# Moving the combination of two attention maps to GpSimd, and delaying the last two gate sigmoids

## The chip, the cores and the metric

The kernel runs on one core of one Trainium2 chip. The metric is the device time of one launch in microseconds (us). Three runs of the kernel before took 1290.82, 1292.57 and 1293.42 us; the median, 1292.57 us, is what the changed kernel is set against.

Five engines matter. PE (TensorE) multiplies matrices into PSUM, with its weight loads shown as PEld. DVE (VectorE), ACT (ScalarE) and POOL (GpSimd) do the elementwise work. SP (SyncE) issues most of the DMAs. Each engine works through its own queue in order, and waits on semaphores that other engines or DMAs raise.

## The reference

One decoder block on x of 1024 tokens by 1024 channels, in float32. The part that the change touches:

```
z = rms_norm(x) @ w_in            -> p, q, k, v, gate_a, gate_b
for each of 4 heads, each block of 128 queries:
    s1 = q1 k1^T * scale + bias ; s2 = q2 k2^T * scale + bias   (causal)
    a  = softmax(s1) - lam * softmax(s2)
    o  = a @ v                                   (v: 128 columns)
    o  = o * rsqrt(mean(o^2) + eps) * subln_g * (1 - lambda_init)
ya = pool_mixer(p) @ w_branch_a ; yb = o_all_heads @ w_branch_b
m  = sigmoid(gate_a) * ya + sigmoid(gate_b) * yb
h  = x + rms_norm(m @ w_out)      then a SwiGLU feed-forward layer
```

## The kernel before, in words

Each float32 matrix product is made of three products of rounded halves (high by high, high by low, low by high); `triple` (lines 230 to 234) issues the three. The high half is an ACT cast, the low half a DVE or POOL subtraction (`sub`, line 87; `load_w`, line 97, uses POOL for the weights of the first branch).

The input projection comes first. It leaves q, k, v, the pooled activations and the gates in DRAM. The gates of channels 128d to 128d+127 are finished by `gate_done` (lines 511 to 519): a sigmoid on ACT for each half of the tokens, then a store from ACT's queue to `sgd[0][d]` (gate_a) or `sgd[1][d]` (gate_b). The last of the eight gate units, d = 7 (`KD - 1`), is not run at once. It becomes the first part of a *filler*: a generator whose steps are three matmuls each, and which goes on with the first branch (`branch(0, ...)`, pooled values by `w_branch_a`).

Attention runs over 32 entries, a head and a block of queries each, in the order of `seq` (line 712). The first three heads alternate long and short blocks (7, 0, 6, 1, 5, 2, 4, 3), the last goes down from 7 to 0. An entry of block qb has maps of 128 x L, L = 128 (qb + 1). It has three parts:

- `scores` (lines 599 to 633). For each of the two maps: matmuls into a PSUM pair; a DVE instruction (line 622) that adds the bias, writes the map `E` to SBUF and gives its row maximum; an exponential on ACT in place (line 625), whose accumulator gives the row sums. Then three DVE instructions (lines 629 to 631) take the reciprocals of the two sums, a factor cf from them, and `E[0] += cf * E[1]`.
- `transposes` (lines 638 to 652). PE transposes the 128 x 128 blocks of E[0] into PSUM (line 646); ACT and DVE make the two halves `AT` (lines 648 and 649).
- `values` (lines 654 to 669). PE multiplies by V (line 660); ACT and DVE scale the two column halves by the reciprocal of the first sum and add them (lines 665 to 667); ACT takes the sum of squares.

`head_norm` (lines 673 to 684) makes the head's norm factor on DVE and POOL (`rstd_of`, lines 121 to 126, a power of -0.5 on POOL) and multiplies on DVE (line 679). `turn_head` (lines 686 to 695) transposes the result for the second branch.

The loop at line 731 issues scores four entries ahead of the values, and transposes one ahead. After each step, `step` (lines 720 to 729) adds a pace to `owed` and issues that many filler steps. Outside the blocks marked `manual_schedule` the framework's scheduler then orders each engine's instructions from this order and from modelled durations; the result is fixed in each engine's queue.

`branch` (lines 576 to 592) takes 128 output channels (d) and 512 tokens (t) at a time: a gate load on SP into a temporary (line 587; two rotating buffers for each of the tags `ft` and `sg`), twelve matmuls into one of two PSUM banks (`fil`), then `take`. `take_a` multiplies by the gate into `ma`; `take_b` (lines 761 to 764) multiplies by the gate and adds `ma`. After the second branch the eight loads of `w_out` (line 776) are on SP too, with casts on ACT (line 777) and subtractions on DVE; they share two `wraw` buffers with the branch weights.

The long-lived tiles come from two pools: `a8` with 16 slots, and `b4` with 14 slots, which holds among others the maps E, the tiles AT and the four O.

Of the kernel before, what the change touches and what calls it, by code (L numbers as in the profile page):

```python
# [10 lines left out]
F32 = mybir.dt.float32  # L11
F32R = mybir.dt.float32r
AF = mybir.ActivationFunctionType
ALU = mybir.AluOpType

P = 128
S = 1024
D = 1024
NB = S // P
KD = D // P  # L20
HALF = 512
NH = 4
# [5 lines left out]
EPS = 1e-6  # L28
# [11 lines left out]
def block_kernel(ctx, tc, x, w_in, pool_mix, pool_scale, w_branch_a, lam_q1, lam_k1, lam_q2,  # L40
                 lam_k2, subln_g, w_branch_b, w_out, mix_pre_g, mix_post_g, ffn_pre_g, ffn_post_g,
                 w_ffn_gate, w_ffn_up, w_ffn_down, out):
    nc = tc.nc
    x, out = x[0], out[0]
# [7 lines left out]
    cp = ctx.enter_context(tc.tile_pool(name="cp", bufs=1))  # L52
# [8 lines left out]
    def name(s):  # L61
        uid[0] += 1
        return f"{s}_{uid[0]}"
# [4 lines left out]
    def b4(shape, dt, s):  # L68
        return sb.tile(shape, dt, tag="b4", bufs=B4, name=name(s))
# [4 lines left out]
    def fil(s):  # L74
        return ps.tile([P, HALF], F32, tag="fil", bufs=2, name=name(s))
# [4 lines left out]
    def small(n, s):  # L80
        return sm.tile([P, n], F32, tag="small", bufs=20, name=name(s))
# [31 lines left out]
    make_identity(nc, ident)  # L113
    mhalf = cp.tile([P, 8], F32, name="mhalf")
    nc.vector.memset(mhalf, -0.5)
    junk = cp.tile([P, D], mybir.dt.bfloat16, name="junk")
    psc = cp.tile([P, 4], F32, name="psc")
    sgc = cp.tile([P, 1], F32, name="sgc")
# [2 lines left out]
    def rstd_of(ss, n, width):  # L121

        t, r = small(n, "ms"), small(n, "rstd")
        nc.vector.tensor_scalar(t, ss, 1.0 / width, EPS, op0=ALU.mult, op1=ALU.add)
        nc.gpsimd.tensor_tensor(out=r, in0=t, in1=mhalf[:, :n], op=ALU.pow)
        return r
# [33 lines left out]
    def tt(o, a, b, op):  # L160
        nc.vector.tensor_tensor(out=o, in0=a, in1=b, op=op)  # L161
# [85 lines left out]
    def temp(s):  # L247
        if s in ("p1", "p5", "c11"):
            return sm.tile([P, HALF], F32, tag="ft", bufs=2, name=name(s))
        return sm.tile([P, HALF], F32, tag="sg", bufs=2, name=name(s))  # L250
# [43 lines left out]
    sgd = [[dr.tile([P, S], F32, name=name("sgd")) for _ in range(KD)] for _ in range(2)]  # L294

    def half(t):
        return slice(t * HALF, (t + 1) * HALF)
# [62 lines left out]
    with tc.manual_schedule(engines={nc.scalar.engine, nc.vector.engine, nc.gpsimd.engine}):  # L360
# [10 lines left out]
        o = [(fil("q"), fil("k")), (mm("q"), mm("k"))]  # L371
# [5 lines left out]
        for tb in range(NB):  # L377
            t, cols = tb // 4, slice(tb % 4 * P, (tb % 4 + 1) * P)
# [43 lines left out]
    for t in range(2):  # L422
        o = (fil("q"), fil("k")) if t == 0 else (mm("q"), mm("k"))
# [13 lines left out]
    lsum, lexp, nlam = small(2, "lsum"), small(2, "lexp"), cp.tile([P, 1], F32, name="nlam")  # L437
# [73 lines left out]
    def gate_done(d):  # L511
        st, seen = [b4([P, S], F32, "g_st") for _ in range(2)], [0, 0]

        def done(e, t, src):
            nc.scalar.activation(st[e][:, half(t)], src, AF.Sigmoid)
            seen[e] += 1
            if seen[e] == 2:
                nc.scalar.dma_start(sgd[e][d], st[e])
        return done
# [13 lines left out]
    heads, attends = {}, {}  # L533
# [42 lines left out]
    def branch(e, w, mov, take):  # L576

        order = [(d, t) for d in range(KD) for t in range(2)]
        if e == 1:
            order[:4] = [(0, 1), (1, 1), (0, 0), (1, 0)]  # L580
        ws = {}
        for d, t in order:
            if d not in ws:
                ws[d] = load_w(w[:, d * P:(d + 1) * P], 4, P, "wb", e == 0)
            bh, bl = ws[d]
            sg = temp(("p1", "sg")[t])
            nc.sync.dma_start(sg, sgd[e][d][:, half(t)])
            o = fil("branch")
            for k in range(4):
                triple(o, bh[:, k, :], bl[:, k, :], *mov(t, k), k == 0, k == 3, False)  # L590
                yield
            take(d, t, o, sg)

    ma = []

    def take_a(d, t, o, sg):
        tt(ma[t][d // 4][:, d % 4, :], o, sg, ALU.mult)

    def scores(h, qb):

        QA, QB, K, V = heads[h]
        slope = 0.25 ** (h + 1)
        L = P * (qb + 1)
        nj = 1 if L <= HALF else 2
        w = L // nj
        q = slice(qb * P, (qb + 1) * P)
        if nj == 1:
            E = b4([P, 2, HALF], F32, "E")
            E = [E[:, 0, :L], E[:, 1, :L]]
        else:  # L610
            E = [b4([P, S], F32, "E")[:, :L] for _ in range(2)]
        nm, sums = small(2, "nm"), small(2, "sums")
        dv = negd[:, S - L:S].rearrange("p (j w) -> p j w", j=nj)
        for m in range(2):
            sc = pair("s")
            for j in range(nj):
                c = slice(j * w, (j + 1) * w)
                nc.tensor.matmul(sc[:, j, :w], QA[:, m, q], K[:, m, c], start=True, stop=False)
                nc.tensor.matmul(sc[:, j, :w], QB[:, m, q], K[:, m, c], start=False, stop=True)
            e = E[m].rearrange("p (j w) -> p j w", j=nj)  # L620

            nc.vector.tensor_tensor_reduce(out=e, in0=sc[:, :nj, :w], in1=dv, scale=-slope,
                                           scalar=3.0e38, op0=ALU.add, op1=ALU.min,
                                           accum_out=nm[:, m:m + 1])
            nc.scalar.activation(E[m], E[m], AF.Exp, bias=nm[:, m:m + 1], scale=-1.0,
                                 accum_out=sums[:, m:m + 1])
            yield
        rec, cf = small(2, "rec"), small(1, "cf")
        nc.vector.reciprocal(rec, sums)
        nc.vector.tensor_scalar(cf, sums[:, 0:1], rec[:, 1:2], nlam, op0=ALU.mult, op1=ALU.mult)  # L630
        nc.vector.scalar_tensor_tensor(out=E[0], in0=E[1], scalar=cf, in1=E[0], op0=ALU.mult, op1=ALU.add)
        attends[h, qb] = E[0], rec
        yield

    O = [b4([P, NB, P], F32, "O") for _ in range(NH)]
    oss = [cp.tile([P, NB], F32, name=name("oss")) for _ in range(NH)]

    def transposes(h, qb):
        E, rec = attends[h, qb]
        ats = []  # L640
        for b0 in range(0, qb + 1, 4):
            n = min(4, qb + 1 - b0)
            pt = mm("aT")
            for i in range(n):
                b = b0 + i
                nc.tensor.transpose(pt[:, i * P:(i + 1) * P], E[:, b * P:(b + 1) * P], ident)
            AT = b4([P, 2, HALF], F32R, "AT")
            nc.scalar.copy(AT[:, 0, :n * P], pt[:, :n * P])
            sub(AT[:, 1, :n * P], pt[:, :n * P], AT[:, 0, :n * P])
            ats.append(AT)  # L650
            yield
        attends[h, qb] = ats, rec

    def values(h, qb):
        V = heads[h][3]
        ats, rec = attends[h, qb]
        o = mm("o")[:, :2 * P]
        for b in range(qb + 1):
            for j in range(2):
                nc.tensor.matmul(o, ats[b // 4][:, j, b % 4 * P:(b % 4 + 1) * P], V[:, b, :, :],  # L660
                                 start=b == 0 and j == 0, stop=b == qb and j == 1)
            if b == 3:
                yield
        ov = O[h][:, qb, :]
        nc.scalar.mul(ov, o[:, P:], rec[:, 0:1])
        nc.vector.scalar_tensor_tensor(out=ov, in0=o[:, :P], scalar=rec[:, 0:1], in1=ov,
                                       op0=ALU.mult, op1=ALU.add)
        sumsq(ov, oss[h][:, qb:qb + 1])
        yield

# [1 line left out]

    def head_norm(h, b=slice(0, NB)):
        n = b.stop - b.start
        r = rstd_of(oss[h][:, b], n, P)

        def scale():
            o = O[h][:, b, :]
            nc.vector.tensor_tensor(out=o, in0=o, in1=r.unsqueeze(2).to_broadcast([P, n, P]), op=ALU.mult)

        if h < NH - 1:
            defer(LAG, scale)
        else:
            scale()
# [46 lines left out]
    for i in range(-AHEAD, len(seq)):  # L731
        j = i + AHEAD
        if j < len(seq):
            h, pos = divmod(j, len(QORDER))
# [7 lines left out]
        if i >= 0:  # L742
            step(values(*seq[i]))
            h, pos = divmod(i, len(QORDER))
# [5 lines left out]
            elif h == NH - 1 and pos % 4 == 3:  # L750
                b = slice(4, 8) if pos == 3 else slice(0, 4)
# [6 lines left out]


    m = [[b4([P, 2, HALF], F32, "m") for _ in range(KD // 2)] for _ in range(2)]  # L760
    def take_b(d, t, o, sg):
        md = m[t][d // 2][:, d % 2, :]
        tt(md, o, sg, ALU.mult)
        tt(md, md, ma[t][d // 4][:, d % 4, :], ALU.add)

    for _ in branch(1, w_branch_b, quad_mov(OT), take_b):
        pass
# [130 lines left out]
    with tc.manual_schedule(engines={nc.tensor.engine, nc.scalar.engine, nc.vector.engine, nc.gpsimd.engine}):  # L898
        o = [fil("wo") for _ in range(2)]
# [9 lines left out]
        og, ss, ms, r = b4([P, D], F32, "og"), small(4, "hss"), small(4, "ms"), small(2, "rstd")  # L909
# [32 lines left out]
        for c in (c0, c1):  # L942
            nc.vector.scalar_tensor_tensor(out=xr[:, c], in0=og[:, c], scalar=r[:, 0:1], in1=xr[:, c],
                                           op0=ALU.mult, op1=ALU.add)
# [8 lines left out]
        for c in (c0, c1):  # L953
            nc.vector.scalar_tensor_tensor(out=og[:, c], in0=xr[:, c], scalar=r[:, 1:2], in1=gpre[:, c],
                                           op0=ALU.mult, op1=ALU.mult)
        sg = temp("sg")
# [22 lines left out]
    sg = temp("sg")  # L979
# [135 lines left out]
    for n, (i, kb) in enumerate(stream):  # L1115
# [8 lines left out]
        o = (Y, X, Y, X, Y, Z, Y)[i]  # L1124
# [40 lines left out]
```

## Time and profile before

| | us |
|---|---|
| median of three runs | 1292.57 |
| the profiled execution, its own time | 1293.83 |
| the span of its trace, first to last instruction | 1292.0 |
| PE busy, of the span | 1248.5 (97%) |
| DVE busy | 836.6 (65%) |
| ACT busy | 581.8 (45%) |
| POOL busy | 139.0 (11%) |

The attention stage, with the filler in it, lies at about 339 to 515 us of the span; the second branch follows until about 554 us, then the output projection and the feed-forward layer. Matmuls are pipelined and their ends are modelled, so PE counts as busy for some time after it could have taken the next matmul. A row of a busy view names line, engine, operation, output and inputs, shape and count, then busy time and the mean of one in ns, then the idle time of the engine just before and what ended it. A row of waits gives the total in us, how many, and the longest. A row of the timeline gives start, duration, engine, line, and in brackets how long the engine had been idle before and what ended that.

### The profile page before, as it was taken

The page shows a single profiled execution, that of the slowest core. Times are in us where ns is not written, and L with a number is a line of the kernel's source. Part 1 is how long each engine was busy: PE and PEld are TensorE (multiplying, and loading weights), DVE is VectorE, ACT ScalarE, POOL GpSimd, SP SyncE. Part 2 cuts the span into 40 slices and gives each one's busy share as a digit, 9 for nine tenths or more (in the row PEclk, how much of TensorE's full clock was granted, in tenths as well). Part 3 has the DMA queues.
Part 4 walks back from the last instruction along what each step waited for, and adds up shares of the span by engine and source line. Part 5 has one row for each costly group of instructions (what it writes and reads, how often), then busy time and mean ns, then how long its engine had stood idle before and what let it go on. Part 6 is the DMA issues. An engine that isn't in the chain of part 4 may idle for free.

```text
span 1292.0 us, 15663 instructions
## 1 busy us (share of the span) xinstructions
PE 1248.5 (97%) x5856; PEld 1038.3 (80%) x5856; DVE 836.6 (65%) x1303; ACT 581.8 (45%) x1033; POOL 139.0 (11%) x129
## 2 busy tenths in 40 slices
PE   4899999999989999999999999999999999999997
PEld 4788778888778887878878888888888888888886
DVE  4866685454369988655599565565566538865666
ACT  6444335344486666244564333333333334444542
POOL 3100000000101001001102111111110111000221
PEclk9899999999999999999999999999999999999999
DMA  7245246432598421543333323233223258733235
GB/s 248 66 159 183 100 152 197 131 118 86 173 307 221 139 73 43 168 160 131 112 106 114 105 91 101 96 122 123 86 86 114 98 197 307 242 101 91 89 107 203
DMA packets 139788, 179.16 MB, mean 139 GB/s; under 512 B 8000, under 2 KB 94528, under 8 KB 137280
## 3 DMA queue, kind: packets, MB, share of 16 engines
q1 hardware_dynamic: 127776, 146.56, 36.0%
q10 hardware_dynamic: 11936, 31.60, 6.3%
q8 instruction: 46, 0.75, 0.2%
q14 instruction: 30, 0.25, 0.1%
HBM read 124.39 MB, written 53.74 MB: 138 GB/s over the span
## 4 chain that ended last, share of the span: by engine, by line
PE 82%; DVE 7%; ACT 4%; DMA 3%; issue 2%; POOL 1%; ACTq 0%; SPq 0%; DVEq 0%; POOLq 0%
PE Y L232 9%; PE Y L233 9%; PE Y L234 9%; PE X L232 5%; PE X L233 5%; PE X L234 5%; PE Yd L233 3%; PE Yd L234 3%; PE Yd L232 3%; PE Z L233 2%; PE Z L234 2%; PE Z L232 2%; PE wo L818 2%; PE wo L819 2%; PE wo L817 2%
## 5 line engine op out<-in xcount | busy, mean ns | idle before, releaser
L161 DVE TENSOR_TENSOR p<-Z,p 128x512 f32<-128x512 f32 x35 | 24.2, 691 | 158.4 <-PE Z L234 158.4
L233 PE MATMUL Y<-A_lo,Wh 128*128 128x512 f32 x296 | 115.7, 391 | 0.3 <-DVE A_lo L87 0.3
L232 PE MATMUL Y<-A_hi,Wh 128*128 128x512 f32 x296 | 115.3, 390 | 0.0
L234 PE MATMUL Y<-A_hi,Wl 128*128 128x512 f32 x296 | 115.1, 389 | 0.0
L232 PE MATMUL Y<-S_hi,Wh 128*128 128x512 f32 x280 | 109.2, 390 | 0.0
L232 PE MATMUL X<-S_hi,Wh 128*128 128x512 f32 x280 | 109.1, 389 | 0.1
L233 PE MATMUL Y<-S_lo,Wh 128*128 128x512 f32 x280 | 109.1, 390 | 0.0
L234 PE MATMUL Y<-S_hi,Wl 128*128 128x512 f32 x280 | 109.1, 390 | 0.0
L234 PE MATMUL X<-S_hi,Wl 128*128 128x512 f32 x280 | 109.0, 389 | 0.0
L233 PE MATMUL X<-S_lo,Wh 128*128 128x512 f32 x280 | 109.0, 389 | 0.0
L201 ACT CAST Wh<-wf_t 128x1024 fp32r<-128x1024 f32 x70 | 72.8, 1053 | 69.2 <-PE X L233 30.7
L87 DVE TENSOR_TENSOR w_op<-wd,w_op 128x512 fp32r<-128x512 f32 x77 | 56.4, 732 | 55.2 <-ACT w_op L165 55.2
L87 DVE TENSOR_TENSOR Wl<-wf_t,Wh 128x1024 fp32r<-128x1024 f32 x70 | 86.6, 1244 | 4.6 <-ACT Wh L201 4.6
L201 ACT CAST Wh<-w_raw 128x1024 fp32r<-128x1024 f32 x72 | 60.6, 843 | 63.1 <-PE Z L233 41.9
L165 ACT CAST w_op<-wd 128x512 fp32r<-128x512 f32 x77 | 47.9, 622 | 89.1 <-PE Yd L234 34.4
L87 DVE TENSOR_TENSOR Wl<-w_raw,Wh 128x1024 fp32r<-128x1024 f32 x72 | 69.6, 966 | 14.5 <-ACT Wh L201 14.5
L233 PE MATMUL Yd<-w_op,s_op 128*128 128x512 f32 x176 | 68.7, 390 | 0.2 <-DVE w_op L87 0.2
L232 PE MATMUL Yd<-w_op,s_op 128*128 128x512 f32 x176 | 68.6, 390 | 0.0
L234 PE MATMUL Yd<-w_op,s_op 128*128 128x512 f32 x176 | 68.3, 389 | 0.0
L161 DVE TENSOR_TENSOR wf_t<-w_raw,wf_t 128x512 f32<-128x512 f32 x70 | 65.7, 938 | 1.0
L233 PEld LDWEIGHTS Y<-A_lo,Wh 128*128 128x128 f32 x296 | 55.6, 188 | 11.9 <-DVE A_lo L87 0.7
L232 PEld LDWEIGHTS Y<-A_hi,Wh 128*128 128x128 f32 x296 | 55.6, 188 | 11.6
(259 smaller groups left out, 3050.5 us busy)
## 6 DMA issues: line engine op xcount, KB each, us to landing
s_raw<-fsd SPq DMA_DIRECT2D x35, 512.0 KB, 3.7
w_raw<-in_w_in_dram SPq DMA_DIRECT2D x32, 512.0 KB, 4.0
w_raw<-in_w_ffn_gate_dram SPq DMA_DIRECT2D x22, 512.0 KB, 3.6
w_raw<-in_w_ffn_up_dram SPq DMA_DIRECT2D x22, 512.0 KB, 3.7
fsd<-fss SPq DMA_DIRECT2D x11, 1024.0 KB, 3.8
wd<-in_w_ffn_down_dram SPq DMA_DIRECT2D x44, 256.0 KB, 5.1
fsd<-F SPq DMA_DIRECT2D x33, 256.0 KB, 2.2
qkd<-qk_st ACTq DMA_DIRECT2D x16, 512.0 KB, 3.5
```

What stands on the lines that cost most here:

```text
L87: nc.vector.tensor_tensor(out=o, in0=a, in1=f32(hi), op=ALU.subtract)
L161: nc.vector.tensor_tensor(out=o, in0=a, in1=b, op=op)
L165: nc.scalar.copy(hi, a)
L201: nc.scalar.copy(hi, a)
L232: nc.tensor.matmul(o, ah, bh, start=start, stop=False, skip_group_check=goes_on)
L233: nc.tensor.matmul(o, ah, bl, start=False, stop=False, skip_group_check=goes_on)
L234: nc.tensor.matmul(o, al, bh, start=False, stop=stop, skip_group_check=goes_on)
L817: nc.tensor.matmul(o[e], mh[:, k, :], wh, start=k == 0, stop=False)
L818: nc.tensor.matmul(o[e], mh[:, k, :], wl, start=False, stop=False)
L819: nc.tensor.matmul(o[e], ml[:, k, :], wh, start=False, stop=k == KD - 1)
```

## The change

Combining the maps goes from DVE to POOL, in four instructions: a product for cf, a power of -1 for the reciprocal of the second sum, a multiplication of E[1] by both, an addition to E[0]. The values are no longer divided by the first sum; the sums are kept for each head (`esum`), and the norm takes eps times the squared first sum instead of eps, which gives the same normed result.

The last gates (d = 7) are stored as they are, by an ACT copy. The first branch does not load its gate for d = 7 and copies its product to `ma` on ACT. The second branch loads both gates for d = 7, takes both sigmoids on ACT in the temporaries, and multiplies `ma` by the first gate on DVE before the addition.

```diff
+    mone = cp.tile([P, 1], F32, name="mone")
+    nc.vector.memset(mone, -1.0)
...
         def done(e, t, src):
-            nc.scalar.activation(st[e][:, half(t)], src, AF.Sigmoid)
+            if d < KD - 1:
+                nc.scalar.activation(st[e][:, half(t)], src, AF.Sigmoid)
+            else:
+                nc.scalar.copy(st[e][:, half(t)], src)
...
-            sg = temp(("p1", "sg")[t])
-            nc.sync.dma_start(sg, sgd[e][d][:, half(t)])
+            gates = []
+            for i in ((0, 1) if d == KD - 1 else (e,)):
+                if d == KD - 1 and e == 0:
+                    continue
+                sg = temp(("p1", "sg")[t ^ (i != e)])
+                nc.sync.dma_start(sg, sgd[i][d][:, half(t)])
+                if d == KD - 1:
+                    nc.scalar.activation(sg, sg, AF.Sigmoid)
+                gates.append(sg)
...
-            take(d, t, o, sg)
+            take(d, t, o, gates)
...
-    def take_a(d, t, o, sg):
-        tt(ma[t][d // 4][:, d % 4, :], o, sg, ALU.mult)
+    def take_a(d, t, o, gates):
+        mad = ma[t][d // 4][:, d % 4, :]
+        if gates:
+            tt(mad, o, gates[0], ALU.mult)
+        else:
+            nc.scalar.copy(mad, o)
...
-        nm, sums = small(2, "nm"), small(2, "sums")
+        nm, sums = small(2, "nm"), esum[h][:, qb, :]
...
-        rec, cf = small(2, "rec"), small(1, "cf")
-        nc.vector.reciprocal(rec, sums)
-        nc.vector.tensor_scalar(cf, sums[:, 0:1], rec[:, 1:2], nlam, op0=ALU.mult, op1=ALU.mult)
-        nc.vector.scalar_tensor_tensor(out=E[0], in0=E[1], scalar=cf, in1=E[0], op0=ALU.mult, op1=ALU.add)
-        attends[h, qb] = E[0], rec
+        cf, rec = small(1, "cf"), small(1, "rec")
+        nc.gpsimd.tensor_tensor(out=cf, in0=sums[:, 0:1], in1=nlam, op=ALU.mult)
+        nc.gpsimd.tensor_tensor(out=rec, in0=sums[:, 1:2], in1=mone, op=ALU.pow)
+        nc.gpsimd.tensor_scalar(E[1], E[1], rec, cf, op0=ALU.mult, op1=ALU.mult)
+        nc.gpsimd.tensor_tensor(out=E[0], in0=E[0], in1=E[1], op=ALU.add)
+        attends[h, qb] = E[0]
...
-        nc.scalar.mul(ov, o[:, P:], rec[:, 0:1])
-        nc.vector.scalar_tensor_tensor(out=ov, in0=o[:, :P], scalar=rec[:, 0:1], in1=ov,
-                                       op0=ALU.mult, op1=ALU.add)
+        nc.scalar.copy(ov, o[:, P:])
+        tt(ov, o[:, :P], ov, ALU.add)
...
-        r = rstd_of(oss[h][:, b], n, P)
+        s0, t, r = esum[h][:, b, 0], small(n, "ms"), small(n, "rstd")
+        nc.vector.scalar_tensor_tensor(out=t, in0=s0, scalar=EPS, in1=s0, op0=ALU.mult, op1=ALU.mult)
+        nc.vector.scalar_tensor_tensor(out=t, in0=oss[h][:, b], scalar=1.0 / P, in1=t, op0=ALU.mult, op1=ALU.add)
+        nc.gpsimd.tensor_tensor(out=r, in0=t, in1=mhalf[:, :n], op=ALU.pow)
...
-    def take_b(d, t, o, sg):
-        md = m[t][d // 2][:, d % 2, :]
-        tt(md, o, sg, ALU.mult)
-        tt(md, md, ma[t][d // 4][:, d % 4, :], ALU.add)
+    def take_b(d, t, o, gates):
+        md, mad = m[t][d // 2][:, d % 2, :], ma[t][d // 4][:, d % 4, :]
+        tt(md, o, gates[-1], ALU.mult)
+        if len(gates) > 1:
+            tt(mad, mad, gates[0], ALU.mult)
+        tt(md, md, mad, ALU.add)
```

More of the change, by code (lines that the diff above doesn't have):

```diff
@@ L627, in scores @@
             yield
-        rec, cf = small(2, "rec"), small(1, "cf")
-        nc.vector.reciprocal(rec, sums)
-        nc.vector.tensor_scalar(cf, sums[:, 0:1], rec[:, 1:2], nlam, op0=ALU.mult, op1=ALU.mult)
-        nc.vector.scalar_tensor_tensor(out=E[0], in0=E[1], scalar=cf, in1=E[0], op0=ALU.mult, op1=ALU.add)
-        attends[h, qb] = E[0], rec
+        cf, rec = small(1, "cf"), small(1, "rec")
[4 more added lines that the diff above has]
+        attends[h, qb] = E[0]
         yield
+    esum = [cp.tile([P, NB, 2], F32, name=name("esum")) for _ in range(NH)]
     O = [b4([P, NB, P], F32, "O") for _ in range(NH)]
@@ L638, in transposes @@
     def transposes(h, qb):
-        E, rec = attends[h, qb]
+        E = attends[h, qb]
         ats = []
@@ L651, in transposes @@
             yield
-        attends[h, qb] = ats, rec
+        attends[h, qb] = ats
     def values(h, qb):
         V = heads[h][3]
-        ats, rec = attends[h, qb]
+        ats = attends[h, qb]
         o = mm("o")[:, :2 * P]
```

## The prediction

> **What bounds the kernel now.** I read the page first. It says that PE is the bound over the whole kernel, so an edit that takes work off DVE or ACT can only pay where PE waits for them.
>
> ```profile
> PE 1248.5 (97%) x5856; PEld 1038.3 (80%) x5856; DVE 836.6 (65%) x1303; ACT 581.8 (45%) x1033; POOL 139.0 (11%) x129
> ```
>
> The windows view then cuts out the attention stage and some stretches of it (columns: stretch, length, busy time of PE, PEld, DVE, ACT, POOL with counts, PE clock, DMA share, GB/s).
>
> ```profile
> 339.00:515.00 176.00, 167.13 (x974) 142.15 (x973) 142.21 (x351) 120.59 (x310) 21.00 (x15) 1.00 0.56 169
> ```
>
> ```profile
> 370.00:380.00 10.00, 8.45 (x49) 6.46 (x47) 5.86 (x15) 9.91 (x21) 0.93 (x1) 1.00 0.83 252
> 380.00:390.00 10.00, 7.57 (x44) 6.26 (x45) 8.97 (x27) 7.27 (x22) 1.04 (x1) 1.00 0.66 237
> 430.00:440.00 10.00, 8.17 (x52) 6.61 (x49) 9.01 (x26) 7.17 (x23) 0.00 (x0) 1.00 0.36 128
> 450.00:460.00 10.00, 10.00 (x59) 8.63 (x58) 9.56 (x27) 7.22 (x22) 1.31 (x1) 1.00 0.25 81
> ```
>
> PE idles 176.00 - 167.13 = 8.87 us in this stage, and 1.55 + 2.43 + 1.83 = 5.81 of it in three of these stretches: the first has ACT full, the others DVE near full. At 450 to 460, DVE is just as busy and PE loses nothing. So the prize is not DVE's share but these idle times, which PE's waits name:
>
> ```profile
> PE s L618 <- DVE nm L622: 3.0, 5, 1.0
> PE oT L692 <- DVE O L679: 1.3, 2, 0.9
> PE aT L646 <- DVE AT L87: 0.9, 2, 0.5
> PE aT L646 <- DVE O L666: 0.9, 2, 0.5
> ...
> PE o L660 <- DVE AT L87: 0.6, 1, 0.6
> PE o L660 <- DVE O L666: 0.5, 1, 0.5
> ```
>
> Those on steps that a freer DVE or ACT brings forward (L622, AT, L666) are 3.0 + 0.9 + 0.9 + 0.6 + 0.5 = 5.9 us in 11 waits. A wait costs a little more than it shows:
>
> ```profile
> 366.70 0.39 PE L233 MATMUL branch<-y2l,wb_hi 128*128 128x512 f32 x1
> 366.93 0.39 PE L234 MATMUL branch<-y2h,wb_lo 128*128 128x512 f32 x1
> ```
>
> Starts are 0.23 us apart while each matmul counts 0.39 as busy, so each wait hides 0.16 us more: 11 x 0.16 = 1.8. The most that the attention part can give is 7.7 us.
>
> **DVE loses the combination.** In the stage (group rows; last figures are busy us and mean ns):
>
> ```profile
> L631 DVE SCALAR_TENSOR_TENSOR E<-E,cf,E 128x1024 f32<-128x1024 f32 (+3 forms) x16 | 17.8, 1114 | 0.0
> L631 DVE SCALAR_TENSOR_TENSOR E<-E,cf 128x128 f32<-128x128 f32 (+3 forms) x16 | 8.7, 545 | 0.1
> L630 DVE TENSOR_SCALAR cf<-sums,rec,nlam 128x1 f32<-128x1 f32 x32 | 8.6, 269 | 0.7
> L629 DVE RECIPROCAL rec<-sums 128x2 f32<-128x2 f32 x32 | 5.2, 162 | 14.7 <-ACT E L625 14.1
> ```
>
> That is 40.3 us off 142.21, leaving about 102 in 176. The additions in `values` keep shape and place and are costed at nothing, as is the early memset, which lies beside the first loads.
>
> **ACT loses table loads.** The gate sigmoids of the filler fall between exponentials:
>
> ```profile
> L625 ACT ACT_TABLE_LOAD x5 | 6.4, 1283 | 0.1
> L515 ACT ACT_TABLE_LOAD x4 | 5.1, 1283 | 0.1
> ```
>
> Stored unscaled, the gates need no sigmoid table here: four loads at L515 and four of five at L625 go, 8 x 1.283 = 10.3 us, all around 356 to 376 us. The chain from there to PE is in the waits of SP's queue and in the timeline:
>
> ```profile
> SPq L549 <- DMA sgd<-g_st: 6.5, 1, 6.5
> ```
>
> ```profile
> 374.29 0.33 ACTq L518 DMA_DIRECT2D sgd<-g_st  x1
> 378.63 0.38 SPq L587 DMA_DIRECT2D p<-sgd  x1
> 388.63 0.69 DVE L161 TENSOR_TENSOR ma<-branch,p 128x512 f32<-128x512 f32 x1
> 390.11 0.39 PE L232 MATMUL branch<-y2h,wb_hi 128*128 128x512 f32 x1
> ```
>
> The late gate store holds SP 6.5 us before a load of QB, the branch's gate loads queue behind it, the first product into `ma` comes at 388.63, and only then is a branch bank free. Late filler and a full ACT leave PE nothing to put between the attention waits of 370 to 390. So the table loads' 10.3 us are not a term of their own: they open 370 to 390, the combination opens 430 to 440. I take three quarters of 7.7, a gain of 5.8 us, because what is late next, the head loads (DMA share 0.83 at 370 to 380), moves only in part.
>
> **POOL gains it.** Nearest rows:
>
> ```profile
> L97 POOL TENSOR_TENSOR wb_lo<-wb_raw,wb_hi x8: 1290/1302/2203, 341.3 to 469.0; 128x512 fp32r<-128x512 f32 x8
> ```
>
> ```profile
> L884 POOL TENSOR_TENSOR fss<-F 128x512 f32<-128x512 f32 x11 | 18.0, 1635 | 181.9 <-DVE F L161 181.9
> L125 POOL TENSOR_TENSOR rstd<-ms,mhalf 128x1 f32<-128x1 f32 x15 | 8.6, 571 | 120.3 <-DVE ms L124 90.9 <-ACT A_hi L798 22.6 <-DVE cnt L450 6.8
> L568 POOL TENSOR_SCALAR_AFFINE_SELECT negd<-negd 128x1024 f32<-128x1024 f32 x1 | 1.0, 1044 | 0.1
> ```
>
> The addition lies between 1302/512 = 2.54 and 1635/512 = 3.19 ns an element. I take 2.54, for the reason in the next paragraph. The multiplication by two scalars isn't in the trace: from 1044/1024 = 1.02 ns (one tile read, affine select) to 2.54 (two tiles read). I take 1.02, since it too reads one tile. The power is 0.57 us, the small product up to that, taken at 0.3. Over 4 heads x 128 x (1 + ... + 8) = 18,432 elements a partition: 47 + 19 + 32 x 0.87 = 94 us, which with the 21.0 already there is 115 of 176. The longest entry takes 0.87 + 1.04 + 2.60 = 4.5 us after its exponential. Is that covered? A tight 1024-wide entry, sums to first transposition:
>
> ```profile
> 429.76 0.19 ACT L625 ACTIVATION_READ_ACCUMULATOR E<-E,nm 128x1 f32 x1
> 437.41 0.66 PE L646 MATMUL aT<-ident,E 128*128 128x128 f32 x4 [0.45 <-DVE AT L87]
> ```
>
> 437.41 - 429.95 = 7.5 us, and PE's wait there is on AT. So 3.0 us stay in hand, and the combination costs nothing while POOL is free. The new waits: POOL stands on each exponential with the branch's `wb_lo` and the head's power behind it; DVE's L679 stands on that power with L622 and AT behind it; E[1]'s buffer comes free some 3 us later. None lies on PE's path within that slack.
>
> The Trainium skill, GPSIMD Engine Reference, section Engine selection, says that elementwise work belongs on VectorE, GpSimd being about twice as slow with two inputs. The rows agree (1302 ns, against 690 for DVE in the row below). By that rule alone the edit adds time; the slack is why I don't forecast that, and the first rival is the case where the rule decides.
>
> Do the two engines slow each other? Two combinations of 896 columns, the first beside a POOL subtraction:
>
> ```profile
> 404.04 1.29 POOL L97 TENSOR_TENSOR wb_lo<-wb_raw,wb_hi 128x512 fp32r<-128x512 f32 x1 [22.99 <-ACT wb_hi L95]
> 404.54 1.73 DVE L631 SCALAR_TENSOR_TENSOR E<-E,cf,E 128x896 f32<-128x896 f32 x1
> 438.35 1.14 DVE L631 SCALAR_TENSOR_TENSOR E<-E,cf,E 128x896 f32<-128x896 f32 x1
> ```
>
> Beside POOL it took 1.73, else 1.14. The Trainium skill's same page (Key points) gives the rule: the two share an SBUF interface, which binds when DVE reads two SBUF inputs. The change itself takes away L631, DVE's main instruction of that kind here; the others mostly read PSUM. So I price POOL undisturbed.
>
> **The second branch and the end.** For d = 7, two more gate loads, four sigmoids, one table load and two products appear, at:
>
> ```profile
> L515 ACT ACTIVATE g_st<-p x16: 631/632/634, 220.4 to 364.4; 128x512 f32<-128x512 f32 x16
> ```
>
> ```profile
> 547.26 0.69 DVE L161 TENSOR_TENSOR m<-m,ma 128x512 f32<-128x512 f32 x1
> 550.75 1.05 ACT L777 CAST woh<-wo_raw 128x1024 fp32r<-128x1024 f32 x1 [2.68 <-DMA wo_raw<-in_w_out_dram]
> 557.00 0.49 PE L817 MATMUL wo<-woh,mh 128*128 128x512 f32 x1 [1.19 <-ACT woh L777]
> ```
>
> That is 4 x 0.63 + 1.28 = 3.8 us on ACT and 2 x 0.69 = 1.4 on DVE, where the `w_out` loads pass through both before PE goes on. SP queues the gate loads ahead of later `w_out` loads, and ACT's sigmoids stand on those loads with the casts behind them. The cost is between nothing (ACT idles 2.68 before a cast there) and 5.2; I take 1.0, because a product can go ahead as soon as its gate is there. The first branch swaps two DVE products for two ACT copies and drops two loads: nothing beside the attention's matmuls, 2 x 0.63 at most without them. The norm's second small DVE instruction lies on the last heads' waits (L679): 2 x 0.16 (as L629) = 0.3.
>
> **Sum.** -5.8 + 1.0 + 0.3 = -4.5. The profiled execution took 1293.83, so 1289.3 in its terms; it is 1.26 over the median, so 1288.1 us against 1292.57.
>
> **Rivals.** *POOL becomes the bound (slower).* The entries need POOL over the time of the exponentials:
>
> ```profile
> L625 ACT ACTIVATE E<-E,nm x64: 386/771/1157, 353.1 to 503.0; 128x1024 f32<-128x1024 f32 x8, 128x128 f32<-128x128 f32 x8, 128x896 f32<-128x896 f32 x8, 128x256 f32<-128x256 f32 x8
> ```
>
> These are 150 us. POOL's other work there is 20 (21.0 less the affine select), the small instructions 32 x 0.87 = 28. If multiplication and addition together cost more than (150 - 20 - 28)/18,432 = 5.5 ns an element (I took 3.56), POOL saturates, the 3 us of slack go, and PE waits for every long entry. At 2.54 + 3.19 = 5.73 POOL needs 153.4 us: the gain is lost, 3.4 us come on top and the 1.3 of the end: 1297.3. For it: the unmeasured multiplication. Against: the affine select at 1.02.
>
> *A wash.* The waits close but others open: PE reaches the head loads too early, and `wo_raw` gets stuck in SP's queue behind gate loads that wait for a buffer. A gain of 2 against a loss of 2: about 1292.5. For it: DMA share 0.83 above, and the wait of 1.19 at 557.00. Against: gate store and head loads move forward too.
>
> *More is won.* All 7.7 us and nothing lost at the end: 1284.9.
>
> **Chances.** Forecast 0.55, wash 0.24, POOL bound 0.16, more won 0.05. A measurement here tells about 0.2% (2.6 us) from no change. The forecast, with its gain at 2 to 6, lies mostly below 1290.0: faster 0.55 + 0.05, less 0.03 that falls inside, 0.57. Same: the wash, 0.24 + 0.03, less 0.03 that overshoots, 0.24. Slower 0.19. The range goes from just below the most that can be won, 1283.5, to just above the POOL rival's price, 1298.
>
> **What would show it.** Right: eight table loads fewer in the stage; DVE near 102 us; POOL near 115, its multiplication near 1.0 us and its addition near 2.6 at 1024 wide; PE idle under 5 us in the stage; 370 to 390 nearly full. Wrong: PE waiting on POOL at L646; a POOL multiplication above 2.5 us at 1024; PE's wait before the first product of L817 grown from 1.19 us by more than 2.

## The result, and the profile after

The changed kernel takes 1290.67 us (median of 13 runs, 1288.29 to 1291.93); the kernel before, on the same chip, 1292.32 us (13 runs, 1290.82 to 1295.01). The ratio is 0.9984 with an interval of 0.9976 to 0.9992: 2.1 us less, within the 0.2% that the prediction called no change. A second set of runs gave 0.9984 again. The forecast was 4.5 us less: the sign holds, the size is about half.

The profiled executions overstate it. The one of before (1293.83) lies above its median, the one of after (1288.29) is the fastest of its 13. And kernels whose code ahead of the attention is the same start it anywhere between 342.3 and 345.8 us in their profiles. The stage itself is steadier: from the first matmul of the scores to the last of the second branch (timeline), before took 207.9 us (343.8 to 551.7), after 204.3 (343.5 to 547.8), after's second profile 205.3.

The page of after: DVE gave up 31 us, POOL took 96, ACT gave up 10.

```profile
PE 1244.3 (97%) x5856; PEld 1036.4 (81%) x5856; DVE 805.9 (63%) x1213; ACT 571.7 (44%) x1032; POOL 235.3 (18%) x257
```

The windows view of after, for the stage and the stretches that the prediction named (length; busy PE, PEld, DVE, ACT, POOL; clock; DMA share; GB/s):

```profile
339.00:515.00 176.00, 168.25 (x990) 145.19 (x989) 114.20 (x262) 108.88 (x305) 115.96 (x143) 1.00 0.57 168
370.00:380.00 10.00, 10.00 (x65) 9.12 (x64) 6.30 (x19) 6.52 (x22) 6.49 (x10) 1.00 0.87 229
380.00:390.00 10.00, 7.11 (x47) 5.68 (x46) 5.22 (x15) 6.12 (x19) 6.66 (x9) 1.00 1.05 320
430.00:440.00 10.00, 10.00 (x68) 9.02 (x67) 7.31 (x22) 5.96 (x20) 8.98 (x10) 1.00 0.01 2
440.00:450.00 10.00, 8.24 (x51) 6.80 (x49) 6.16 (x15) 6.79 (x21) 9.54 (x12) 1.00 0.25 79
```

The two holes that were to be filled are filled: 370 to 380 and 430 to 440 show PE full. But the stretch behind each has opened: 380 to 390 went from 7.57 to 7.11, and 440 to 450 shows 8.24, where it was full before:

```profile
440.00:450.00 10.00, 10.00 (x63) 8.95 (x64) 9.53 (x23) 6.06 (x20) 2.92 (x2) 1.00 0.33 105
```

PE's idle time in the whole stage went from 8.87 to 7.75 only; the prediction looked for less than 5. The waits of PE in the stage of after:

```profile
PE o L678 <- DVE AT L87: 2.0, 2, 1.7
PE branch L236 <- POOL wb_lo L97: 1.5, 1, 1.5
PE s L634 <- DVE nm L638: 1.0, 1, 1.0
PE oT L712 <- DVE O L699: 1.0, 1, 1.0
PE oT L712 <- DVE nm L638: 0.9, 1, 0.9
PE aT L664 <- DVE AT L87: 0.6, 2, 0.4
```

The prices on POOL (mean ns behind the busy time):

```profile
L647 POOL TENSOR_SCALAR E<-E,rec,cf 128x1024 f32<-128x1024 f32 x4 | 4.8, 1210 | 0.4
L648 POOL TENSOR_TENSOR E<-E,E 128x1024 f32<-128x1024 f32 x4 | 9.6, 2410 | 0.2
L646 POOL TENSOR_TENSOR rec<-esum,mone 128x1 f32<-128x1 f32 x32 | 18.7, 586 | 12.6 <-ACT E L641 10.5 <-DVE ma L163 2.0
L645 POOL TENSOR_TENSOR cf<-esum,nlam 128x1 f32<-128x1 f32 x32 | 7.1, 223 | 14.8 <-ACT E L641 14.7
```

### The profile page after: what moved, and what is told of

Same layout as the page of the kernel before. It is cut to its first block, busy times and chain, and to the rows that moved or that the text cites. A ratio compares the mean times of both kernels' runs of the same rounds, so it can differ in the third digit from the quotient of the medians.

```text
span 1286.5 us, 15805 instructions
## 1 busy us (share of the span) xinstructions
PE 1244.3 (97%) x5856; PEld 1036.4 (81%) x5856; DVE 805.9 (63%) x1213; ACT 571.7 (44%) x1032; POOL 235.3 (18%) x257
## 4 chain that ended last, share of the span: by engine, by line
PE 83%; DVE 6%; DMA 4%; issue 2%; ACT 2%; POOL 2%; ACTq 0%; DVEq 0%; SPq 0%; POOLq 0%
PE Y L234 10%; PE Y L235 10%; PE Y L236 10%; PE X L234 5%; PE X L235 5%; PE X L236 5%; PE Yd L235 3%; PE Yd L236 3%; PE Yd L234 3%; PE Z L236 2%; PE Z L235 2%; PE Z L234 2%; PE o L678 2%; PE branch L236 2%; PE branch L234 2%
## 5 line engine op out<-in xcount | busy, mean ns | idle before, releaser
L97 POOL TENSOR_TENSOR wb_lo<-wb_raw,wb_hi 128x512 fp32r<-128x512 f32 x8 | 11.3, 1408 | 303.4 <-DVE Wl L87 301.7
```

The costliest lines, as they stand in the source:

```text
L97: nc.gpsimd.tensor_tensor(out=lo, in0=raw, in1=f32(hi), op=ALU.subtract)
```

## The experiments

Each kernel ran beside the kernel before on the same chip, and the ratio is against that. The runs fall into three groups, in which the medians of before were 1293.19, 1292.54 and 1292.29 us, so 0.001 of a ratio is 1.3 us.

**Which part carries it?** Theory A: the table loads around 370 us are worth the gain. Theory B: relieving DVE of the combination is. The first experiment keeps only the gates' part of the change.

```diff
# e1_gates_only, against the changed kernel
-        cf, rec = small(1, "cf"), small(1, "rec")
...
-        nc.gpsimd.tensor_tensor(out=E[0], in0=E[0], in1=E[1], op=ALU.add)
-        attends[h, qb] = E[0]
+        rec, cf = small(2, "rec"), small(1, "cf")
+        nc.vector.reciprocal(rec, sums)
...
+        attends[h, qb] = E[0], rec
```

> Only the gate part of the change; the combination stays on DVE and the values stay scaled. Theory A (the gain comes from the eight table loads that leave ACT at 356 to 376 us): 2 to 4 us under the kernel before, PE nearly full at 370 to 390. Rival B (the gain comes from DVE, which no longer combines the maps; the gates give at the front what they take in the second branch): within 1 us of the kernel before, DVE still about 140 us busy in the attention stage.

Measured: 0.9972 (0.9963 to 0.9982), 3.6 us less than before.

The second keeps only the combination, with unscaled outputs and the new norm:

```diff
# e2_combine_only, against the changed kernel
-            if d < KD - 1:
-                nc.scalar.activation(st[e][:, half(t)], src, AF.Sigmoid)
-            else:
-                nc.scalar.copy(st[e][:, half(t)], src)
+            nc.scalar.activation(st[e][:, half(t)], src, AF.Sigmoid)
...
-            take(d, t, o, gates)
+            take(d, t, o, sg)
```

> Only the combination part: GpSimd combines, values unscaled, gates as before with their sigmoids between the exponentials. Theory A: within 1 us of the kernel before, since ACT still carries eight table loads and PE still idles at 370 to 390. Rival B: 1.5 to 3 us under the kernel before, with PE's waits on L622's successor gone at 430 to 440.

Measured: 0.9954 (0.9941 to 0.9966), 6.0 us less. Each part alone beats the whole: 3.6 and 6.0 us against 2.1. Neither A nor B says that. The lengths of the stage, measured as above, agree: 205.1 us with the gates alone and 202.3 with the combination alone, where before had 207.9 and the whole change 204.3. PE's idle time by windows shows where the parts collide. One fence each, for before, gates alone, combination alone, and the whole change:

```profile
370.00:390.00 20.00, 16.01 (x93) 12.72 (x92) 14.83 (x41) 17.18 (x42) 1.97 (x1) 1.00 0.75 245
430.00:460.00 30.00, 28.17 (x171) 24.19 (x169) 28.10 (x74) 20.45 (x62) 4.22 (x3) 1.00 0.32 105
```

```profile
370.00:390.00 20.00, 18.52 (x115) 15.31 (x114) 15.35 (x40) 13.85 (x42) 1.28 (x1) 1.00 0.78 243
430.00:460.00 30.00, 28.45 (x180) 24.89 (x179) 27.30 (x72) 20.37 (x60) 4.22 (x3) 1.00 0.24 78
```

```profile
370.00:390.00 20.00, 17.44 (x106) 14.35 (x105) 12.89 (x32) 17.56 (x47) 14.28 (x22) 1.00 0.81 262
430.00:460.00 30.00, 30.00 (x186) 26.79 (x186) 22.59 (x56) 21.87 (x63) 26.38 (x34) 1.00 0.15 46
```

```profile
370.00:390.00 20.00, 17.11 (x110) 14.79 (x109) 11.52 (x31) 12.63 (x40) 13.15 (x18) 1.00 0.96 275
430.00:460.00 30.00, 28.24 (x173) 24.71 (x172) 21.43 (x54) 20.99 (x60) 25.95 (x29) 1.00 0.15 45
```

From 370 to 390 us, PE idles 3.99 before; the gates alone leave 1.48, the combination alone 2.56, both together 2.89. So what the parts win there doesn't add: together they leave more than either alone. The gates alone lose 1.20 again at 391, in one wait on the row maximum. From 430 to 460 the combination alone closes all 1.83, the whole change 0.07 of it.

The third puts the combination back on DVE and keeps the rest of the change:

```diff
# e3_all_but_pool, against the changed kernel
-        nc.gpsimd.tensor_tensor(out=cf, in0=sums[:, 0:1], in1=nlam, op=ALU.mult)
-        nc.gpsimd.tensor_tensor(out=rec, in0=sums[:, 1:2], in1=mone, op=ALU.pow)
-        nc.gpsimd.tensor_scalar(E[1], E[1], rec, cf, op0=ALU.mult, op1=ALU.mult)
-        nc.gpsimd.tensor_tensor(out=E[0], in0=E[0], in1=E[1], op=ALU.add)
+        nc.vector.reciprocal(rec, sums[:, 1:2])
+        nc.vector.tensor_scalar(cf, sums[:, 0:1], rec, nlam, op0=ALU.mult, op1=ALU.mult)
+        nc.vector.scalar_tensor_tensor(out=E[0], in0=E[1], scalar=cf, in1=E[0], op0=ALU.mult, op1=ALU.add)
```

> The whole change, but the combination in its unscaled form stays on DVE (reciprocal, factor, one scalar_tensor_tensor). Theory A: 2 to 4 us under the kernel before, so no worse than the changed kernel. Rival B: within 1 us of the kernel before, DVE near 140 us busy in the stage.

Measured: 0.9998 (0.9986 to 1.0009). It differs from the first experiment by the unscaled values and the norm alone, and the gain of 3.6 us is gone. From the changed kernel (0.9984) it differs by the engine of the combination alone, so that POOL's part is worth some 1.8 us there, with intervals that overlap a little. Its waits show two that the first has not, of AT and of a weight's low half:

```profile
PE o L677 <- DVE AT L87: 1.0, 1, 1.0
PE branch L236 <- POOL wb_lo L97: 0.9, 1, 0.9
```

So small edits change where PE waits for AT and for the weight conversion, with or without POOL, and 1 to 3 us go with that. That the order which the scheduler chose is the cause is argued and not shown, since no run held it fixed.

The fourth leaves out the four late sigmoids, so that the raw gates are multiplied in:

```diff
# e4_no_late_sigmoid, against the changed kernel
                 nc.sync.dma_start(sg, sgd[i][d][:, half(t)])
-                if d == KD - 1:
-                    nc.scalar.activation(sg, sg, AF.Sigmoid)
                 gates.append(sg)
```

> The changed kernel with the second branch's four late sigmoids left out (the last gates are used unsquashed). If their 3.8 us on ACT lie partly on the path to the output projection, as the prediction's term of 1.0 says: about 1 us under the changed kernel, 2.7 under the kernel before. If they are hidden: as the changed kernel, 1.7 under the kernel before. If the whole of it is on the path: 5 under the kernel before.

Measured: 0.9982 (0.9974 to 0.9991), against 0.9984: no cost of the late sigmoids shows, though the intervals leave room for some 1.5 us. The timeline of after fits that: the table load and the sigmoids run while PE multiplies for the second branch, and the first product with `w_out` (second row) has no wait in front of it.

```profile
538.16 1.28 ACT L598 ACT_TABLE_LOAD   x1
...
547.59 0.39 PE L839 MATMUL wo<-woh,mh 128*128 128x512 f32 x1
```

In before the first product had none either:

```profile
551.56 0.39 PE L817 MATMUL wo<-woh,mh 128*128 128x512 f32 x1
```

The 1.19 us that the prediction shows at 557.00 stood before a later product. Of such waits, up to 566 us, before shows 1.19 and 0.77, after 0.29, 0.74 and 0.35.

**Is the interference real, and what is it made of?** Two kernels run again: the changed one and the combination alone.

> The changed kernel as it is, beside the combination alone on the same chip. The two parts gave 3.6 us (gates) and 6.0 us (combination) alone, and some 2 together. Theory C (the parts get in each other's way, so the difference is real): 1.5 to 3 us under the kernel before, and at least 2 us above the combination alone. Rival D (it was the chip and the hour): within 1.5 us of the combination alone.

> Only the combination part, once more. Theory C: 5 to 7 us under the kernel before. Rival D: within 1.5 us of the changed kernel.

Measured: 0.9984 (0.9973 to 0.9996) and 0.9956 (0.9944 to 0.9968). The interference is real. Then the wait for `wb_lo` at 446 us. In after (timeline), ACT casts the branch weights at 443.15, POOL is busy with a map's addition (L648) until 444.8, and PE stands:

```profile
443.15 0.61 ACT L95 CAST wb_hi<-wb_raw 128x512 fp32r<-128x512 f32 x1
444.84 1.27 POOL L97 TENSOR_TENSOR wb_lo<-wb_raw,wb_hi 128x512 fp32r<-128x512 f32 x1
446.16 0.50 PE L236 MATMUL branch<-y2h,wb_lo 128*128 128x512 f32 x1 [1.47 <-POOL wb_lo L97]
```

In the combination alone, the order has that cast 18 us earlier, and there is no such wait:

```profile
424.97 0.63 ACT L95 CAST wb_hi<-wb_raw 128x512 fp32r<-128x512 f32 x1
```

The next kernel takes the low half off POOL:

```diff
# e6_wb_lo_on_dve, against the changed kernel
-                ws[d] = load_w(w[:, d * P:(d + 1) * P], 4, P, "wb", e == 0)
+                ws[d] = load_w(w[:, d * P:(d + 1) * P], 4, P, "wb")
```

> The changed kernel with the low half of the first branch's weights made on DVE, so that it no longer queues behind the combinations on GpSimd. If PE's wait of 1.5 us for it at 446 us is a standing cost of the busy GpSimd queue: 1 to 2 us under the changed kernel. If another wait takes its place: as the changed kernel.

Measured: 0.9997 (0.9987 to 1.0006), no gain over the changed kernel; the intervals are too wide to call it a loss. The wait is gone, and PE is nearly full from 440 to 450 (9.72 of 10), but another, 0.35 us in the changed kernel, has grown to 1.85 at 413.61, and behind it the granted clock drops (third value from the right: 0.83):

```profile
413.61 0.50 PE L678 MATMUL o<-V,AT 128*128 128x256 f32 x2 [1.85 <-DVE AT L87]
```

```profile
410.00:420.00 10.00, 8.15 (x43) 7.05 (x42) 6.57 (x14) 5.16 (x17) 7.85 (x10) 0.83 0.64 148
```

This wait is of the edit's own making. On DVE, one of the low halves began while POOL was in an addition and took 2.29 us, where the median of the ten in this stage is 0.69, and AT stands behind it:

```profile
410.57 1.83 POOL L648 TENSOR_TENSOR E<-E,E 128x768 f32<-128x768 f32 x1
410.66 2.29 DVE L87 TENSOR_TENSOR wb_lo<-wb_raw,wb_hi 128x512 fp32r<-128x512 f32 x1
```

So this kernel swaps one hold-up for another, and leaves open how much of the 3.6 us between the whole change and the combination alone is the wait at 446. The next kernel goes at the other collision. With the combination alone, it asks for the first four gate loads ahead of the next head's loads:

```diff
# e7_gates_first, against the combination alone
+        for d, t in ((0, 0), (0, 1), (1, 0), (1, 1)):
+            early[d, t] = gate(0, d, t)
         for _ in load_head(1):
...
```

(The lines left out make the first branch use these loads in place of its own.)

> The combination part alone, with the first four gate loads of the first branch issued ahead of the loads of the second head. Theory E (the filler stands still until about 390 us because these gate loads wait behind 4 MB of head loads on saturated DMAs): the first product into ma comes before 380 us, PE is full at 380 to 390, and the time is 1 to 3 us under the combination alone. Rival F (PE's idle time there is the attention's own, or the head loads that now land later take its place): within 1 us of the combination alone.

Measured: 1.0020 (1.0011 to 1.0029), slower than before. The first product into `ma` came at 384.80 us, earlier than the 388.00 of the combination alone but not before 380, and 380 to 390 filled from 8.66 to 9.48. It was lost again later: DVE's scaling of O waited for the head's power, which stood on POOL behind a map; behind the scaling PE waited 2.24 us; and then the clock was at a half for seven:

```profile
436.99 1.22 DVE L693 TENSOR_TENSOR O<-O,rstd 128x1024 f32<-128x1024 f32 x1 [1.66 <-POOL rstd L689]
438.48 0.55 PE L658 MATMUL aT<-ident,E 128*128 128x128 f32 x3 [2.24 <-DVE O L163]
```

```profile
440.00:450.00 10.00, 8.85 (x33) 6.88 (x32) 2.39 (x5) 2.86 (x8) 6.54 (x8) 0.71 0.27 76
```

**How much slack has POOL?** The prediction had POOL cost nothing until it saturates, at 150 us of work. Two kernels add multiplications by one, which leave the values as they are: one to each entry, then two.

```diff
# e8_pool_more, against the changed kernel (e9_pool_full adds the line twice)
         nc.gpsimd.tensor_scalar(E[1], E[1], rec, cf, op0=ALU.mult, op1=ALU.mult)
+        nc.gpsimd.tensor_scalar(E[1], E[1], 1.0, 1.0, op0=ALU.mult, op1=ALU.mult)
         nc.gpsimd.tensor_tensor(out=E[0], in0=E[0], in1=E[1], op=ALU.add)
```

> The changed kernel with one more GpSimd multiplication of E[1] by 1.0 in each entry: at the 0.85 ns an element and 0.34 us each of its own trace some 27 us more, so GpSimd near 142 us busy of the 150 of the exponentials. If the prediction's slack holds (the combination costs nothing until GpSimd is full): within 1.5 us of the changed kernel, 2 under the kernel before. If GpSimd is on the path already: 5 to 27 us above the changed kernel.

> The changed kernel with two more such multiplications, some 53 us: 169 us of work for 150. If GpSimd binds from 5.5 ns an element on, as the prediction's rival says (here some 6.4 with the fixed parts): 10 to 20 us above the changed kernel, PE waiting on GpSimd before the transpositions. If the entries' slack still covers it: within 1.5 us.

Measured: 1.0087 (1.0074 to 1.0101) and 1.0197 (1.0181 to 1.0213). Against the changed kernel (0.9984) that is 13 and 27 us more, for 21.6 and 43.2 us of added POOL work. The rows of the first, its added line and its stage, show POOL at 137 of 176 us, far from full:

```profile
L648 POOL TENSOR_SCALAR E<-E 128x1024 f32<-128x1024 f32 (+7 forms) x32 | 21.6, 674 | 2.6
```

```profile
339.00:515.00 176.00, 160.10 (x929) 137.68 (x928) 106.35 (x251) 105.69 (x299) 137.33 (x175) 0.97 0.55 161
```

Its waits, PE's first:

```profile
PE aT L665 <- DVE AT L87: 4.1, 3, 3.5
PE branch L236 <- POOL wb_lo L97: 3.3, 1, 3.3
```

```profile
DVE O L700 <- POOL rstd L696: 9.3, 5, 3.9
```

PE does not wait for the maps here. It waits for what stands behind the maps in POOL's queue: for `wb_lo` directly, and for AT, which stands on DVE behind the scaling of O, which stands on the head's power. With two multiplications more, PE waits for the map itself too (the addition is then at L650):

```profile
PE aT L666 <- POOL E L650: 5.4, 4, 2.3
PE branch L236 <- POOL wb_lo L97: 4.7, 1, 4.7
```

**Does an earlier request for the weights mend it?** The last two ask for the branch weights one d earlier, in the changed kernel and in the combination alone:

```diff
# e10_weights_ahead, against the changed kernel; e11 is the same edit on the combination alone
-            if d not in ws:
-                ws[d] = load_w(w[:, d * P:(d + 1) * P], 4, P, "wb", e == 0)
+            for i in (d, d + 1) if e == 0 else (d,):
+                if i < KD and i not in ws:
+                    ws[i] = load_w(w[:, i * P:(i + 1) * P], 4, P, "wb", e == 0)
```

> The changed kernel with the first branch's weights asked for one group of channels earlier. Theory G (what the whole change loses against the combination alone is PE's wait at 446 us for weights that the scheduler converts one step later than there): that wait goes, 1.5 to 3 us under the changed kernel. Rival H (the wait is only where slack runs out, and another takes its place, as with the weights on DVE): within 1 us of the changed kernel.

> The combination alone with the same earlier weights. Theory G: as the combination alone, 5 to 7 us under the kernel before, for it has no such wait. Rival H: 1 to 3 us either way, from another order alone.

Measured: 0.9988 (0.9979 to 0.9997) and 0.9965 (0.9952 to 0.9977), no gain over 0.9984 and 0.9956. In the first, the wait for `wb_lo` fell from 1.47 to 0.88 only, and the time did not follow. ACT's cast of those weights moved from 443.15 to 442.53, not to the 424.97 of the combination alone, so the edit did not bring about the order that Theory G is about, and the theory stays undecided.

The best version is the combination alone, 0.9954 and 0.9956 in two groups of runs, some 5.8 us under the kernel before and over 3 under the whole change.

## Why the prediction was half right, step by step

**The prices of POOL: right.** The multiplication took 1.21 us at 1024 (1.04 foreseen), the addition 2.41 (2.60), the power 0.59 (0.57), the small product 0.22 (0.3). POOL was busy 115.96 us, foreseen 115.

**DVE near 102: wrong, a mistake of the sum.** It shows 114.20. The 40.3 us were added up from rows, and rows of DVE overlap in time, while the busy time of the windows view counts overlapped time once. All DVE rows of before's stage add up to 164 us, where the busy time is 142.21. A sum of rows can't be taken off a busy time. The sum of the rows itself fell by 35.6 and not 40.3, mainly because the norm's small instructions grew by 5.1 us (below).

**Eight table loads fewer: right.** One is left at the gate sigmoids (L518) and one at the exponentials (L641), where before had five and five; one is added in the second branch.

**"None lies on PE's path within that slack", with a slack of 3.0 us: wrong.** The slack was read at one entry, from the map to its own first transposition. POOL's queue is in order, and what PE came to wait for was not the map but the two things behind it, the weight's low half and the head's power. In after, `wb_lo` is one wait of 1.5 us in a stretch with POOL at 9.54 of 10. The added multiplications show the rest: each us of work on POOL costs about 0.6 us at the end, from where the changed kernel stands (part of it through the clock, below). POOL is at 66% of the stage there.

**The POOL rival: its mechanism is not what happened.** It put the point of decision at 150 us of POOL work. At 137, where it says nothing is lost, 13 us are lost. The rule beside it (the Trainium skill, GPSIMD Engine Reference, Engine selection: elementwise work to VectorE) has the price about right and the outcome wrong for this kernel: POOL needed 31.8 + 14.0 + 26.5 + 18.7 + 7.1 = 98 us for what DVE did in 40.3, and the move still gained some 1.8 us against the third experiment. The combination alone, which has the unscaled values and the new norm with it, gained 6.0, and PE waits there for POOL only 0.3 us of the stage.

**The gain at 370 to 390 and 430 to 440, "three quarters of 7.7": the step that failed.** It gave the first stretch to the table loads and the second to the combination, as two parts of one sum. Each part alone does about that: the gates bring the idle time of 370 to 390 from 3.99 to 1.48, the combination that of 430 to 440 from 1.83 to nothing. Together they leave 2.89 in the first. Of the 5.9 us of waits that were to go, 3.6 are left in after (1.0 on L638, 0.6 and 2.0 on AT), and 1.5 on `wb_lo` and 0.9 on L638 in front of a transposition of O are new.

The longest wait that is left there, 1.67 us at 384.42, is on AT, and the chain to it (critical view of after) runs through ACT and DVE, though neither is near full from 380 to 390 (6.12 and 5.22 of 10). The cast for AT stands on ACT behind the exponentials, and AT on DVE behind the cast:

```profile
381.99 0.89 ACT E L641 x3
...
383.17 0.48 ACT AT L666
...
383.68 0.70 DVE AT L87
```

PE has no filler to put there: no product of the branch starts between 378.64 and 391.63. The gate loads that the branch needs are issued 2 us earlier than before (the first at 376.55, before at 378.63) and land no earlier, since they take 2 us longer (DMA rows of before and of after, 376 to 381 us; last column: us from issue to landing):

```profile
p<-sgd SPq DMA_DIRECT2D x2, 256.0 KB, 6.8
```

```profile
p<-sgd SPq DMA_DIRECT2D x2, 256.0 KB, 8.8
```

The DMA share from 380 to 390 went from 0.66 to 1.05. But the loads don't end last. The first has landed by 385.6, and the first product into `ma` comes at 390.42 (before: 388.63). In DVE's queue it stands behind a row maximum for which DVE itself waits for PE's scores:

```profile
388.18 1.22 DVE L638 CUSTOM_DVE_ANT_0 E<-s,negd 128x1024 f32<-128x1024 f32 x1 [1.31 <-PE s L635]
...
390.42 0.69 DVE L163 TENSOR_TENSOR ma<-branch,p 128x512 f32<-128x512 f32 x1
```

In the kernel with the gates first, the first load was issued at 358.12, took 7.5 us at most, and the product came only at 384.80. So the place in DVE's queue, which the scheduler fixes, holds the branch back, and not the landing; why it chose that place no run shows. The case that the wash named ("PE reaches the head loads too early") is not what happened here. The second stretch opened as foreseen (8.17 to 10.00), and 1.76 of it came back as the idle time of 440 to 450.

**The end, +1.0: not found.** The kernel without the late sigmoids took the same time within the intervals, and the wait of 1.19 us was read as that of the first product, which had none.

**The norm, +0.3:** three of its ten small DVE instructions took 1.5 to 1.7 us instead of 0.16 (below). No run isolates what of it reached the end.

**Which case came true.** The measured -2.1 lies between the forecast and the wash: the sign was right, but the waits closed only in part and others opened, so that the main term of -5.8 shrank to some -2. Two of the signs named for a right prediction did not come: 370 to 390 nearly full (17.11 of 20) and less than 5 us of idle time in the stage.

**What stays open.** Why the unscaled values and the norm alone take away the gain of the gates (third experiment), and how much of the 3.6 us between the combination alone and the whole change is the order of the weight conversion. No kernel moves the combination with the values still scaled and the gates as before, so how much of the 6.0 us is POOL's alone is open too. All kernels that hold the gates' part together with the unscaled values, those with added POOL work aside, show a wait of 0.9 us or more for AT or `wb_lo` somewhere between 384 and 447 us, and no repair that was tried turned into time. An order held fixed by hand, which would separate the edits from what the scheduler makes of them, was not tried.

## What to carry to other kernels

Two edits that work on the same stretch need not add: test each alone before adding their terms, and ask what stands in the queues of the engines next, even where none of them is full. The slack of a step that moves to an in-order engine is the slack of the tightest instruction that will stand behind it in that queue, not of the step itself. Take a difference of busy times from windows of both kernels or from rows of both, never one from the other.

## What the runs showed of the hardware

**A wait can cost twice.** In the kernel with `wb_lo` on DVE, 1.85 us without a matmul were followed by a granted clock of 0.50 from 415.0 to 418.4 us; in the kernel with the gates first, 2.24 us by 0.50 from 439.0 to 445.8. These are one and two times 3.4 us. Shorter waits can do it: two of 1.67 and 1.00 us, 2.3 us apart, are in the profile of after (at 384.42 and 386.72), where the clock stayed at 1.00, and in that of the kernel with one more multiplication (at 384.15 and 386.44), where it was 0.50 from 386.1 to 389.5. It doesn't always follow, even on longer ones: in that kernel a wait of 3.3 us for `wb_lo` near 450 left the clock at 1.00, and one of 3.5 for AT near 485 did not:

```profile
450.00:460.00 10.00, 7.29 (x38) 6.16 (x39) 4.31 (x11) 4.70 (x13) 9.53 (x13) 1.00 0.25 79
```

```profile
484.00:492.00 8.00, 5.61 (x22) 5.17 (x23) 5.36 (x11) 3.20 (x9) 5.89 (x9) 0.57 0.00 0
```

The Trainium skill, TensorE: Matmul & The Clock Gate, Part 1, describes a gate that halves the clock after an idle window, with windows of 3413 ns that run on regardless of when the kernel starts. The length of the drops agrees, and so does the chance in it. Its rule of thumb, no gaps over about 3.4 us, is too generous here: 1.85 was enough. Part of the loss in those two kernels, and of the 0.6 us for each us of POOL, is thus the clock (0.97 over the stage of 176 us with one more multiplication, so at most some 5 of the 13 us, in that profile). It does not explain why the whole change is behind the combination alone: both profiles show 1.00 in all stretches quoted, and the mean granted clock over all their executions is the same, 0.995.

**POOL can hold up a DVE instruction tenfold.** The norm's instruction on eight elements, with two inputs from SBUF, takes 0.16 us when POOL is between two instructions. Where POOL was in an addition of two tiles, it took 1.64 us, and 1.68 and 1.51 in two more places (timeline of after):

```profile
399.30 2.12 POOL L648 TENSOR_TENSOR E<-E,E 128x896 f32<-128x896 f32 x1
399.80 1.64 DVE L693 SCALAR_TENSOR_TENSOR ms<-esum 128x8 f32<-128x8 f32 x1
...
431.12 0.16 DVE L693 SCALAR_TENSOR_TENSOR ms<-esum 128x8 f32<-128x8 f32 x1
```

399.80 + 1.64 = 401.44 and 399.30 + 2.12 = 401.42: it stood until the addition was through. Beside POOL's multiplication of one tile it took 0.17 in the combination alone (at 431.03). In the kernel with the combination on DVE, all ten of these took 0.15 to 0.17. The low half of a weight on DVE, above, with 2.29 us beside an addition, fits this too. The Trainium skill, GPSIMD Engine Reference, Key points, says that the two engines share SBUF interfaces and names DVE instructions with two SBUF inputs; the trace agrees. The prediction priced POOL undisturbed on the ground that DVE's other instructions mostly read PSUM. That held for AT (0.69 us at 512 columns before and after), and not for these ten.
